# One core, a hybrid S5 and attention step: second products in two passes, and FFN heads that start on two of three chunks

## The chip, the cores and the metric

The kernel runs on one core of a Trainium2 chip. The metric is the device time of one execution in microseconds. TensorE (PE in the profile) multiplies, PEld is its weight load, VectorE is DVE, ScalarE is ACT, GpSimd is POOL; SP issues most of the DMAs.

## The reference

Two layers over 1024 latent and 256 context tokens, width 1024. Layer 0 mixes with an S5 state space model, whose result `z` goes through a gated product; layer 1 mixes with attention. Each is followed by a SwiGLU FFN of width 2816, and every sublayer ends in a residual and a LayerNorm:

```python
# S5 mixer, tail
val, gate = jnp.split(z @ w_glu, 2, axis=-1)
(val * jax.nn.sigmoid(gate)) @ w_out
# FFN
gate, up = jnp.split(h @ w_in, 2, axis=-1)
(jax.nn.silu(gate) * up) @ w_out
# around each sublayer
x = layer_norm(alpha * x + gate * sublayer(x * (1 + scale) + shift))
```

Latent tokens attend to latent and cached keys, context tokens to context alone. The outputs are `y`, the new keys and values, and the S5 end states.

## The kernel before, in words

The 1280 tokens lie along the free axis in three chunks, `CH`: chunks 0 and 1 are 512 latent tokens each, chunk 2 is the 256 context tokens. A [1024 x tokens] matrix is eight tiles of 128 partitions. Every product is three matmuls on numbers split in a high part `hi` and a rest `lo` (`mm3`: hi*hi, hi*lo, lo*hi): ACT copies to `hi`, and DVE, or POOL, subtracts to get `lo`. So each operand costs one ACT and one DVE or POOL instruction before PE can use it.

**First products** (S5 GLU, FFN in). The 2*NF output tiles come in gate and up pairs. The first one or two pairs (`ffn_head`) multiply all three chunks plainly, chunk by chunk as the LayerNorm gives them. The rest (`ffn_pair`) use a Winograd scheme on the latent chunks: seven products of 12 matmuls of 512 columns in place of eight, and two context products of 24 matmuls of 256 columns. It needs sums of weight blocks (S1 to S4, `i_step`, DVE) and sums of input tiles (T1 to T4, `x_sums`: a DVE subtraction, an ACT copy and a POOL subtraction, sixteen times). `x_sums` is handed out two or four at a time among the head units from chunk 1 on. Results are spilled to `dI`.

**Second products** (`out_chunks`: S5 out, attention out, FFN out) take three passes, one for each chunk, of eight output tiles `f`; each pass loads and splits all weights again (`w_ahead`), and splits the spilled tiles (`z_ahead`) during its first `f`. After a pass, that chunk's LayerNorm runs as a Python generator whose steps `boundary` emits between later units, by a clock of estimated PE time and the step lengths `YW`. The norm writes `hi` and `lo` of the next input at once (ACT and POOL); then `affine` forms the next residual (ACT for even tiles, POOL for odd), and `keep` stores it with a DMA of the SP queue. The residual tile of a unit is loaded on SP as the unit begins; in the S5 out product ACT scales it at once (`scaled`).

All engines run their instructions in the order in which they are written. Pages (512 columns) come from a pool of 88.

Of the kernel before, what the change touches and what calls it, by code (L numbers as in the profile page):

```python
# [6 lines left out]
F32 = mybir.dt.float32  # L7
# [6 lines left out]
P = 128  # L14
D = 1024
KT = 8
# [593 lines left out]
LL = 2.5  # L610


YW = (2.5, 3, 1, 4, 3.5, 1, 2.6)


class Dense(S5):
# [14 lines left out]
    def out_units(self, ws, tiles, acc, gate, c):  # L631

        v, g = self.nc.vector, self.nc.gpsimd
        n = len(tiles)
        ps = {}

        def mms(f, lo, hi):
            if lo == 0:
                ps[f] = self.psum()[:, :CH[c][1]]
            for i in range(lo, hi):  # L640
                t = tiles[i]
                self.mm3([ps[f]], *(x(P * f) for x in ws(i)), t[0][c:c + 1], t[1][c:c + 1], i == 0, i == n - 1)

        def unit(f, lo=0):
            mms(f, lo, n)
            self.accumulate(acc, gate, f, c, ps.pop(f))
            if f == 2:
                rs = self.rs[c] = self.pgn(CH[c][1])
                g.tensor_tensor(rs, acc[0][c], acc[1][c], op=ALU.add)
            for k in [f - 1] * (f > 2) + [f] * (f == 7):  # L650
                (v if k == 7 else g).tensor_tensor(self.rs[c], self.rs[c], acc[k][c], op=ALU.add)
            return 3 * n * CH[c][1] / 2400

        if c:
            return [lambda f=f: unit(f) for f in range(8)]

        first = [lambda f=f, i=i: mms(f, i, i + 1 + (i == 0)) for i in [0, *range(2, n - 1)] for f in range(4)]
        return first + [lambda f=f: unit(f, n - 1 if f < 4 else 0) for f in range(8)]

# [4 lines left out]


    def glu_plan(self, nt, cs, head, tail):

        ev = []
        done = 2 * head
        body = list(range(nt - tail))  # L670
        for a in range(0, len(body), cs):
            c = body[a:a + cs]

            need = max(done, min(2 * nt, 2 * c[-1] + 3))
            ev += [("in", (k // 2, k % 2)) for k in range(done, need)]
            done = need

            ev.append(((0, 1, 2) if c[-1] + 1 < nt - tail else (0,), c))
        return ev + [("in", (k // 2, k % 2)) for k in range(done, 2 * nt)]

    def glu_weights(self, win, wout, nt, cs, head, tail):
        out = [win[t] for t in range(2 * head)]
        for k, a in self.glu_plan(nt, cs, head, tail):
            out += [win[2 * a[0] + a[1]]] if k == "in" else [wout[t] for t in a]
        return out + [wout[t] for t in self.glu_last(nt, cs, tail)]

    def glu_gate(self, it, c, ps, half, act):

        n = CH[c][1]
        if half == 0:  # L690
            it["s"][c] = self.pgn(n)
            self.nc.scalar.activation(it["s"][c], ps, act)
        else:
            s = it["s"][c]
            self.nc.vector.tensor_tensor(s, s, ps, op=ALU.mult)
            for k in range(2):
                it["hl"][k][c] = self.pgn(n, F32R)
            self.split(it["hl"][0][c], it["hl"][1][c], s)

    def ffn_head(self, hh, hl, head, act, raw):  # L700

        ls, self.LS = self.LS, 0
        ws = [self.w_next() for _ in range(2 * head)]
        self.LS = ls
        s = {}
        sums = []

        def unit(t, half, c):
            n = CH[c][1]
            if c == 1 and t == half == 0:  # L710
                self.x_start(hh, hl, raw)
                sums.append(self.x_sums())
                self.i_load()
            ps = self.gemm(ws[2 * t + half], hh, hl, c)
            if half == 0:
                s[t, c] = self.pgn(n)
                self.nc.scalar.activation(s[t, c], ps, act)
            else:
                x = s.pop((t, c))
                self.nc.vector.tensor_tensor(x, x, ps, op=ALU.mult)  # L720
                self.spill(t, c, x)
            if sums:
                for _ in range(16 // (4 * head)):
                    next(sums[0], None)
            if c == 2:
                self.XC = [(hh[k][2], hl[k][2]) for k in range(KT)]
                self.i_until(2 * t + half + 2)
            return n / 100

        return [[lambda t=t, h=h, c=c: unit(t, h, c) for t in range(head) for h in range(2)] for c in range(3)]  # L730

    def glu_new(self, t):
        self.inter[t] = {"s": [None] * 3, "hl": ([None] * 3, [None] * 3)}
        return self.inter[t]

    def glu_head(self, hh, hl, head, act):

        self.inter = {}
        ls, self.LS = self.LS, 0
        ws = [self.w_next() for _ in range(2 * head)]  # L740
        self.LS = ls
        its = [self.glu_new(t) for t in range(head)]

        def unit(t, half, c):
            self.glu_gate(its[t], c, self.gemm(ws[2 * t + half], hh, hl, c), half, act)
            if c == 2:
                self.w_ahead(min(2 * t + half + 1, ls))
            return CH[c][1] / 100

        return [[lambda t=t, h=h, c=c: unit(t, h, c) for t in range(head) for h in range(2)] for c in range(3)]  # L750

    def glu_last(self, nt, cs, tail):

        return [*range(nt - tail, nt), *range(nt - tail - cs, nt - tail)]

    def glu_body(self, hh, hl, nt, cs, head, tail, act, acc, gate):
        for k, a in self.glu_plan(nt, cs, head, tail):
            if k == "in":
                t, half = a
                self.LS = LL if t == nt - 1 else 2  # L760
                it = self.inter[t] if half else self.glu_new(t)
                w = self.w_next()
                ps = self.gemm_all(w, hh, hl)
                for c in range(3):
                    self.glu_gate(it, c, ps[c], half, act)
            else:
                ws = [self.w_next() for _ in a]
                self.out_all(ws.__getitem__, [self.inter[t]["hl"] for t in a], acc, gate, k)

    def out_all(self, ws, tl, acc, gate, chunks=(0, 1, 2), each=None):  # L770
        for f in range(8):
            ps = [self.psum()[:, :CH[c][1]] for c in chunks]
            for i, t in enumerate(tl):
                rh, rl = ([t[k][c] for c in chunks] for k in range(2))
                self.mm3(ps, *(x(P * f) for x in ws(i)), rh, rl, i == 0, i == len(tl) - 1)
            for c, x in zip(chunks, ps):
                self.accumulate(acc, gate, f, c, x)
# [1317 lines left out]
```

## Time and profile before

| | |
|---|---|
| median of 3 runs (3427.3 to 3431.05) | 3430.57 us |
| the profiled execution's own time | 3426.6 us |
| its span, first to last instruction | 3424.8 us |
| mean granted TensorE clock, share of full speed | 0.965 |
| busy share: PE, PEld, DVE, ACT, POOL | 93%, 79%, 62%, 40%, 14% |

The profile is of one execution. A line such as L121 is the line of the kernel's source; L121, L123 and L125 are the three matmuls of `mm3`, L1079 those of a Winograd product and L1088 those of its context product. In a window the columns are its length, then for each engine the busy time with the number of instructions, then the granted clock of TensorE, the mean DMA share and GB/s.

### The profile page before, as it was taken

To read this page: it belongs to the slowest core of one execution; us is meant where nothing else is said; L and a number is where in the kernel's file an instruction comes from. 1 tells how busy PE (TensorE), PEld (TensorE's weight loads), DVE (VectorE), ACT (ScalarE), POOL (GpSimd) and SP (SyncE) were. 2 spreads that over 40 slices of the span, in tenths; PEclk is the share of its full clock that TensorE was granted. 3 is DMA by queue.
4 is the path that set the end of the run, shared out by engine and by line. 5 is a ranking of instruction groups with operands and counts; after the bars stand their busy time and mean duration, and the time that the engine had idled before them with its cause. 6 is when DMAs were issued, how large, how long until landed. Compare 5 with 4: busy or idle time off the path is not lost.

```text
span 3424.8 us, 47261 instructions
## 1 busy us (share of the span) xinstructions
PE 3199.5 (93%) x17734; PEld 2693.8 (79%) x17734; DVE 2109.5 (62%) x4279; ACT 1384.6 (40%) x2721; POOL 463.6 (14%) x435
## 2 busy tenths in 40 slices
PE   8999689997899999899889999999889999999997
PEld 5763568776788888787778899998678888878777
DVE  7789764475644444445555788887775444454645
ACT  3351442344422222424444477775453222232433
POOL 2230130032400000002122310001350000000000
PEclk9999789998999999999989999999899999999998
DMA  7679952334112121543442200002322121234544
GB/s 256 171 212 328 243 148 72 117 125 153 66 61 80 61 81 57 200 165 120 126 131 76 68 24 16 9 27 87 127 89 82 60 80 60 75 131 142 183 130 147
DMA packets 232998, 392.99 MB, mean 115 GB/s; under 512 B 54992, under 2 KB 111984, under 8 KB 232000
## 3 DMA queue, kind: packets, MB, share of 16 engines
q1 hardware_dynamic: 225280, 365.01, 33.4%
q0 software_dynamic: 7488, 24.96, 2.4%
q8 instruction: 139, 2.28, 0.3%
q14 instruction: 91, 0.75, 0.1%
HBM read 309.14 MB, written 80.74 MB: 114 GB/s over the span
## 4 chain that ended last, share of the span: by engine, by line
PE 74%; DVE 5%; ACT 2%; DMA 2%; issue 1%; POOL 1%; SPq 0%; ACTq 0%; DVEq 0%; POOLq 0%
PE ps L1079 26%; PE ps L123 9%; PE ps L121 9%; PE ps L125 9%; PE ps L1088 8%; PE ps L1478 3%; PE ps L1499 1%; PE ps L1497 1%; PE ps L1498 1%; PE ps L1436 1%; PE ps L1437 1%; PE ps L1438 1%; DVE pg L103 1%; ACT pg L102 1%; DMA pg<-dI 1%
## 5 line engine op out<-in xcount | busy, mean ns | idle before, releaser
L1079 PE MATMUL ps<-pg,pg 128*128 128x512 f32 x3948 | 919.3, 391 | 13.8 <-ACT pg L1102 8.6
L1079 PEld LDWEIGHTS ps<-pg,pg 128*128 128x128 f32 x3948 | 738.8, 189 | 165.5 <-ACT pg L1102 9.9
L121 PE MATMUL ps<-pg,pg 128*128 128x512 f32 (+1 forms) x2112 | 740.6, 370 | 103.1 <-ACT pg L131 65.1
L123 PE MATMUL ps<-pg,pg 128*128 128x512 f32 (+1 forms) x2112 | 731.7, 366 | 7.2 <-DVE pg L132 4.3
L125 PE MATMUL ps<-pg,pg 128*128 128x512 f32 (+1 forms) x2112 | 726.9, 364 | 6.0 <-DVE pg L103 5.9
L121 PEld LDWEIGHTS ps<-pg,pg 128*128 128x128 f32 x2112 | 407.8, 197 | 176.6 <-ACT pg L131 69.6
L123 PEld LDWEIGHTS ps<-pg,pg 128*128 128x128 f32 x2112 | 406.6, 197 | 76.1 <-DVE pg L132 11.9
L125 PEld LDWEIGHTS ps<-pg,pg 128*128 128x128 f32 x2112 | 406.9, 197 | 67.5 <-DVE pg L103 10.4
L103 DVE TENSOR_TENSOR pg<-wr,pg 128x512 fp32r<-128x512 f32 (+1 forms) x444 | 331.0, 788 | 182.2 <-ACT pg L102 178.2
L102 ACT ACTIVATE pg<-wr 128x512 fp32r<-128x512 f32 (+1 forms) x444 | 244.8, 597 | 325.4 <-DMA wr<-in_w_ffn_out 230.1
L1088 PEld LDWEIGHTS ps<-pg,pg 128*128 128x128 f32 x2256 | 283.1, 191 | 7.3
L1088 PE MATMUL ps<-pg,pg 128*128 128x256 f32 x2256 | 285.3, 283 | 0.0
L1204 POOL TENSOR_TENSOR pg<-pg,pg 128x512 f32<-128x512 f32 x8 | 11.6, 1450 | 1418.2 <-DVE pg L662 1336.0
L662 DVE SCALAR_TENSOR_TENSOR pg<-ps,mods,pg 128x512 f32<-128x512 f32 x64 | 47.9, 749 | 233.6 <-PE ps L125 226.3
L1044 DVE TENSOR_TENSOR pg<-pg,pg 128x512 fp32r<-128x512 f32 x188 | 137.8, 733 | 77.4 <-ACT pg L1040 77.4
L132 DVE TENSOR_TENSOR pg<-ps,pg 128x512 fp32r<-128x512 f32 (+1 forms) x210 | 142.0, 677 | 65.1 <-ACT pg L131 59.7
L131 ACT ACTIVATE pg<-ps 128x512 fp32r<-128x512 f32 (+1 forms) x210 | 124.0, 590 | 70.8 <-PE ps L1478 47.6
L1458 ACT ACTIVATE pg<-ps,nb,rq 128x512 f32<-128x512 f32 x192 | 149.0, 777 | 5.7 <-DVE sm L1467 2.6
L1127 DVE TENSOR_TENSOR pg<-pg,ps 128x512 f32<-128x512 f32 x47 | 32.3, 688 | 193.1 <-PE ps L1079 193.1
L1113 DVE TENSOR_TENSOR pg<-pg,ps 128x512 f32<-128x512 f32 x47 | 32.3, 688 | 191.2 <-PE ps L1079 191.2
L1443 DVE TENSOR_REDUCE mx<-ps 128x1 f32<-128x512 f32 (+1 forms) x208 | 137.0, 660 | 1.3 <-PE ps L1438 1.3
L1044 DVE TENSOR_TENSOR pg<-wr,pg 128x512 fp32r<-128x512 f32 x188 | 133.4, 709 | 2.2 <-ACT pg L1040 2.2
(344 smaller groups left out, 4707.3 us busy)
## 6 DMA issues: line engine op xcount, KB each, us to landing
gw<-in_w_mod SPq DMA_DIRECT2D x192, 256.0 KB, 5.2
wr<-in_w_ffn_out SPq DMA_DIRECT2D x96, 512.0 KB, 4.5
wr<-in_w_ffn_in SPq DMA_DIRECT2D x88, 512.0 KB, 4.1
dI<-pg SPq DMA_DIRECT2D x104, 256.0 KB, 4.6
pg<-dI SPq DMA_DIRECT2D x104, 256.0 KB, 5.4
wr<-in_w_ffn_out SPq DMA_DIRECT2D x48, 384.0 KB, 3.6
wr<-in_w_s_out SPq DMA_DIRECT2D x24, 512.0 KB, 3.6
dX<-pg SPq DMA_DIRECT2D x48, 256.0 KB, 2.5
```

The lines of the kernel that those rows point to most:

```text
L102: nc.scalar.activation(hi, x, AF.Copy)
L103: nc.vector.tensor_tensor(lo, x, hi.bitcast(F32), op=ALU.subtract)
L121: mm(ps[c], wh, rh[c], start=first, stop=False)
L123: mm(ps[c], wh, rl[c], start=False, stop=False)
L125: mm(ps[c], wl, rh[c], start=False, stop=last)
L131: self.nc.scalar.activation(hi, src, AF.Copy)
L132: self.nc.vector.tensor_tensor(lo, src, hi.bitcast(F32), op=ALU.subtract)
L1044: v.tensor_tensor(lo, self.isum[i, name], hi.bitcast(F32), op=ALU.subtract)
L1079: mm(ps, p[:, o], q, start=(first and k == 0 and j == 0), stop=(k == 3 and j == 2), skip_group_check=True)
L1088: mm(ps, p[:, o], q, start=(k == 0 and j == 0), stop=(k == KT - 1 and j == 2))
L1443: v.tensor_reduce(mx[:, kc:kc + 1], ps, axis=AX.X, op=ALU.max)
L1458: nc.scalar.activation(p, u["bank"].pop((qt, kc)), AF.Exp, bias=nb[:, 0:1], scale=rq, accum_out=sm[:, kc:kc + 1])
```

## The change

Every GLU and FFN pair is now Winograd (five plain pairs disappear: one in the GLU, two in each FFN). The first `GF` = 2 (GLU) or `FF1` = 3 (FFN) pairs are cut in two: `HEAD` (products P1 and P2, which read chunk 0 alone, and the context products G and U) and `TAIL` (the other five products, which read sums with chunk 1). The weights of such a pair are loaded twice.

Second products run in two passes (`TWO`): chunk 0 with the context, then chunk 1. The last FFN out product keeps three (`ONE`). Tiles are split ahead during the last pair (`last`). Residuals are loaded one `f` earlier, and scaled on ACT just before they are used.

The LayerNorm writes one plain tile; `h_split` splits it later, as do the hooks in the last unit of a pass, half of the `lo` on DVE and half on POOL. The T sums are formed by `x_next` as the first `TAIL` begins. `affine` issues its store on the queue of the engine that computed it (ACT or POOL), in place of SP.

```diff
-YW = (2.5, 3, 1, 4, 3.5, 1, 2.6)
+YW = (2.5, 3, 1, 4, 3.5, 1, 1.6)
...
             if A is not None:
-                t = self.pgn(n)
-                nc.scalar.activation(hh[kt][c], a, AF.Identity, bias=B[:, kt, cd:cd + 1], scale=A[:, kt, cd:cd + 1])
...
+                raw[kt][c] = t
                 if kt % 2:
                     v.tensor_scalar(t, a, A[:, kt, cd:cd + 1], B[:, kt, cd:cd + 1], op0=ALU.mult, op1=ALU.add)
                 else:
                     nc.scalar.activation(t, a, AF.Identity, bias=B[:, kt, cd:cd + 1], scale=A[:, kt, cd:cd + 1])
-                nc.gpsimd.tensor_tensor(hl[kt][c], t, hh[kt][c].bitcast(F32), op=ALU.subtract)
...
+            after(nc.gpsimd, kt, c)
...
+            after(nc.scalar, kt, c)
...
-        for c in range(3):
-            run(outs[c])
+        for units, cs in zip(outs, passes):
+            run(units)
             if not gens:
                 clock[1] = clock[0] + YW[0]
-            gens.append(ln(c, ready))
...
+            gens += [ln(c, ready) for c in cs]
+        for c, units in heads or ():
+            while not ready[c]:
+                clock[1] = clock[0] + step()
+            run(units)
...
+FULL = ("A11", "S1", "S2", "A12", "S3", "A22", "S4", "A21"), ("P1", "P5", "P6", "P2", "P7", "G", "P4", "P3", "U")
+HEAD = ("A11", "A12", "A21", "A22"), ("P1", "P2", "G", "U")
+TAIL = ("S1", "S2", "S3", "S4", "A22"), ("P6", "P5", "P7", "Z3", "P4")
...
+    def h_split(self, kt, c, eng):
...
+        self.nc.scalar.activation(hi, self.xr[kt][c], AF.Copy)
+        eng.tensor_tensor(lo, self.xr[kt][c], hi.bitcast(F32), op=ALU.subtract)
+        self.hs[kt, c] = hi, lo
+
+    def x_next(self, n):
...
+        eng = (v, g)[k % 2]
+        if n == "C":
+            self.h_split(k, 2, eng)
+        elif n[0] == "B":
...
+            self.h_split(kt, c, eng)
...
+            v.tensor_tensor(t, x, y, op=ALU.subtract)
+            self.xt[n, k] = t
+            hi, lo = self.page(F32R), self.page(F32R)
+            nc.scalar.activation(hi, t, AF.Copy)
+            eng.tensor_tensor(lo, t, hi.bitcast(F32), op=ALU.subtract)
+            self.X[n][k] = hi, lo
...
+        self.segs = [(t, HEAD) for t in p[:first]] + [(t, TAIL) for t in p[:first]] + [(t, FULL) for t in p[first:]]
...
+        h0 = [lambda: self.x_all("B11", "B21")] + [u for k, u in U[:2]]
+        h2 = [lambda: self.x_all("C")] + [u for k, u in U[2:]]
+        return [(0, h0), (2, h2)]
+
+    def ffn_body(self, act, first, last):
+        ready = {0: ("T1", "T2"), 1: ("T3",), 2: ("B22",), 3: ("T4",)}
+        for i in range(first, len(self.segs)):
+            for s, kind in enumerate(self.segs[i][1][1]):
+                if i == first:
+                    self.x_all(*ready.get(s, ()))
+                if i == len(self.segs) - 1:
+                    last(s)
+                self.ffn_step(i, kind, act)
...
+        self.zo = [(c, i) for cs in passes for i in range(nk) for c in cs]
...
+                for ps, x in zip(st["ps"], z):
+                    self.mm3([ps], *(y(P * (i - lo)) for y in w), x[:1], x[1:], i == 0, i == nk - 1)
...
+                        while hook and len(hook) > nh * (nk - 1 - i) / nk:
+                            hook.pop(0)()
...
+        TWO, ONE = ((0, 2), (1,)), ((0,), (1,), (2,))
+
+        def keep(eng, kt, c):
             o, n = CH[c]
-            nc.sync.dma_start(self.dX[kt][:, o:o + n], acc[kt][c])
...
+            eng.dma_start(self.dX[kt][:, o:o + n], acc[kt][c])
...
+        def last(s):
+
+            if s > 2:
+                self.z_ahead(2 * (s - 2))
+            if s > 3:
+                self.w_ahead(0.5 * (s - 3))
...
+        def ffn_hook(l):
+            self.x_start(new())
+            self.i_start(L("w_ffn_in", l), range(NF), FF1)
+            return some(0, ("B11", "B21"), 8) + [lambda k=k: self.i_until(k) for k in range(4)] + some(2, ("C",), 8)
...
+            for c in (0, 2, 1):
+                yield c, [lambda: take(c)] + h[c]
```

The last lines are the attention layer's heads: keys and values of chunk 0, then of the context, then of chunk 1, each after `take(c)` has split that chunk.

## Rows read from the trace of the kernel before

**Rows 1.** The page, part 1: busy time, share of the span, instructions of each engine.

```profile
PE 3199.5 (93%) x17734; PEld 2693.8 (79%) x17734; DVE 2109.5 (62%) x4279; ACT 1384.6 (40%) x2721; POOL 463.6 (14%) x435
```

**Rows 2.** Chain in order of time inside one pair: start us, us, what.

```profile
519.36 13.63 PE ps L1079 x60
532.99 2.87 PE ps L1088 x24
535.86 5.47 PE ps L1079 x24
```

**Rows 3.** Windows by stage: length, busy us (instructions) per engine, clock, DMA.

```profile
443.96:668.24 224.28, 210.37 (x1074) 179.12 (x1072) 127.83 (x184) 78.47 (x145) 30.92 (x18) 0.96 0.30 88
720.84:781.89 61.05, 50.91 (x211) 40.43 (x210) 40.92 (x68) 25.63 (x43) 20.77 (x17) 0.92 0.28 95
781.89:827.25 45.36, 32.43 (x211) 29.84 (x210) 30.12 (x61) 21.15 (x43) 5.63 (x8) 0.81 0.52 171
896.46:914.05 17.59, 15.45 (x62) 12.37 (x61) 12.75 (x17) 7.81 (x14) 12.25 (x8) 0.90 0.38 127
1397.22:1407.19 9.97, 0.17 (x3) 0.01 (x1) 2.14 (x20) 0.64 (x2) 0.00 (x0) 0.76 0.99 337
1530.23:1668.84 138.61, 128.88 (x548) 104.03 (x546) 71.16 (x119) 51.88 (x94) 23.61 (x18) 0.96 0.45 145
1668.84:1769.99 101.15, 81.55 (x574) 77.72 (x572) 64.29 (x113) 45.83 (x85) 20.15 (x18) 0.88 0.47 148
1769.99:1833.02 63.03, 58.18 (x382) 53.46 (x381) 37.44 (x79) 26.08 (x56) 17.00 (x19) 0.95 0.16 50
2351.26:2394.91 43.65, 43.65 (x195) 36.12 (x194) 27.14 (x38) 15.76 (x31) 9.64 (x6) 1.00 0.43 145
2394.91:2446.80 51.89, 47.43 (x212) 37.90 (x210) 41.30 (x67) 21.92 (x35) 19.09 (x14) 1.00 0.24 79
3062.83:3069.27 6.44, 0.17 (x3) 0.00 (x1) 0.46 (x3) 0.67 (x2) 0.00 (x0) 0.92 0.98 323
3191.98:3322.87 130.89, 125.07 (x548) 102.08 (x546) 66.03 (x115) 45.12 (x86) 9.33 (x6) 0.99 0.46 149
3322.87:3406.33 83.46, 73.18 (x548) 71.12 (x546) 53.19 (x102) 36.17 (x69) 5.98 (x6) 0.92 0.51 163
```

**Rows 4.** Waits of the SP queue at the stores: total us, times, longest.

```profile
SPq L1621 <- ACT pg L913: 135.8, 14, 22.2
...
SPq L1621 <- ACT hp L913: 77.4, 8, 40.4
```

**Rows 5.** Timeline of the SP queue in the first out product's second chunk.

```profile
770.68 2.26 SPq L1621 DMA_DIRECT2D dX<-pg  x2
773.02 0.38 SPq L1682 DMA_DIRECT2D pg<-in_x  x1
```

**Rows 6.** Timeline of ACT, same place; in brackets the idle time before, and releaser.

```profile
775.93 0.63 ACT L1683 ACTIVATE pg<-pg 128x512 f32<-128x512 f32 x1 [5.28 <-DMA pg<-in_x]
```

**Rows 7.** Timeline of ACT at the start of the S5 layer's GLU.

```profile
455.20 0.63 ACT L131 ACTIVATE pg<-pg 128x512 fp32r<-128x512 f32 x1 [0.34 <-DMA pg<-dZL]
```

**Rows 8.** Timeline of DVE in the GLU's first pairs.

```profile
479.83 2.48 DVE L989 TENSOR_TENSOR pg<-pg,pg 128x512 f32<-128x512 f32 x4
...
488.21 6.52 DVE L991 TENSOR_TENSOR pg<-pg,pg 128x512 f32<-128x512 f32 x4
```

**Rows 9.** Timeline of POOL over the same stretch.

```profile
478.84 22.06 POOL L995 TENSOR_TENSOR pg<-pg,pg 128x512 fp32r<-128x512 f32 x11 [3.90 <-ACT pg L994]
```

**Rows 10.** Groups by line and shape: busy us, mean ns, idle before, releaser.

```profile
L994 ACT ACTIVATE pg<-pg 128x512 fp32r<-128x512 f32 x48 | 28.8, 629 | 37.2 <-DVE pg L991 11.6 <-DVE pg L987 10.8 <-DVE pg L985 10.4
...
L995 POOL TENSOR_TENSOR pg<-pg,pg 128x512 fp32r<-128x512 f32 x48 | 75.2, 1593 | 62.7 <-ACT pg L994 62.7
```

**Rows 11.** Timeline of PE at chunk 2's norm before the first FFN.

```profile
860.01 0.59 PE L857 MATMUL ps<-hp,ones 128*128 128x256 f32 x2
...
880.14 0.58 PE L121 MATMUL ps<-pg,pg 128*128 128x256 f32 x1 [1.15 <-ACT pg L886]
```

More of the change, by code (lines that the diff above doesn't have):

```diff
@@ L629, in gemm_all @@
         return ps
[L631 to L658, printed above, removed]
     def accumulate(self, acc, gate, f, c, ps):
@@ L681, in glu_weights @@
[L681 to L750, printed above, removed]
@@ L770, in out_all @@
[L770 to L777, printed above, removed]
-            if each:
-                each()
@@ L898, in layer_norm @@
         ready[c] = True
-        if A is not None and after:
+        if A is not None:
             for kt in range(KT):
@@ L936, in run @@
                     clock[1] = max(clock[1], clock[0] - 2.0) + step()
-        for c in range(3):
-            run(outs[c])
+        for units, cs in zip(outs, passes):
+            run(units)
             if not gens:
                 clock[1] = clock[0] + YW[0]
-            gens.append(ln(c, ready))
-        hd = heads() if heads else [[], [], []]
-        for c in range(3):
-            if hd[c]:
-                while not ready[c]:
-                    clock[1] = clock[0] + step()
-            run(hd[c])
+            gens += [ln(c, ready) for c in cs]
[3 more added lines that the diff above has]
+            run(units)
         lap = 0
@@ new lines, in x_all, with i_start @@
+    def x_all(self, *names):
+        for n in names:
+            while self.x_next(n):
+                pass
+    def i_start(self, win, pairs, first):
+        self.win = win
+        p = list(pairs)
+        self.segs = [(t, HEAD) for t in p[:first]] + [(t, TAIL) for t in p[:first]] + [(t, FULL) for t in p[first:]]
+        self.items = [(i, n) for i, (_, (names, _)) in enumerate(self.segs) for n in names]
+        self.iraw, self.isum, self.ihi, self.isp, self.il, self.ik, self.iu = {}, {}, {}, {}, 0, 0, 0
+        self.ev = {}
@@ L1216 @@
+            return 3 * (hi - lo) * sum(CH[c][1] for c in cs) / 2220
+        return [[lambda p=p, f=f, o=o: unit(p, f, o) for f in range(8) for o in range(0, nk, 8)] for p in range(len(passes))]
 SHUF = [(i + 16) % 32 for i in range(32)]
@@ L1675, in rest @@
-        self.wseq += self.out_plan(L("w_s5_out"), KT)
-        zh = zl = None
-        body(AF.Sigmoid, KT, self.spilled)
+        self.x_start(zz)
+        for c in (0, 2, 1):
+            zload(c)
+        heads = self.ffn_heads(AF.Sigmoid, GF)
+        for c, units in heads:
+            for u in units:
+                u()
+        self.out_start(KT, TWO, self.spilled)
+        self.wseq += self.out_plan(L("w_s5_out"), KT, 2)
+        self.LS = 1.5
+        self.ffn_body(AF.Sigmoid, GF, last)
@@ new lines, in rest, with heads, take @@
+        self.x_start(new())
+        hooks = [lambda k=k: self.w_ahead(0.5 * k + 0.5) for k in range(8)]
+        outs = self.out_chunks(acc, self.mod(0, 5), NF, TWO, self.residual, None,
+                               some(0, ("B11", "B21"), 8) + hooks + some(2, ("C",), 8))
+        self.wseq += L("w_qk")[:2] + L("w_v") + L("w_qk")[2:]
+        hh, hl = new(), new()
+        def heads():
+            self.at_consts()
+            h = self.at_head(hh, hl)
+            def take(c):
+                for kt in range(KT):
+                    if (kt, c) not in self.hs:
+                        self.h_split(kt, c, (nc.vector, nc.gpsimd)[kt % 2])
+                    hh[kt][c], hl[kt][c] = self.hs[kt, c]
+            for c in (0, 2, 1):
+                yield c, [lambda: take(c)] + h[c]
```

456 lines of the change are left out of this document (204 added, 252 removed).

## The prediction

> **What bounds the kernel now.** First the page: PE is busy 93% of the span, no other engine above 62% (PEld apart) [rows 1]. So I ask what a stage costs over its matmuls. The chain of waits inside a Winograd pair gives the pace: 60 matmuls of 512 columns in 13.63 us are 0.2272 each, 24 of 256 in 2.87 are 0.1196, and a pair is 13.63 + 2.87 + 5.47 + 2.87 = 24.84 us with no gap [rows 2]. In the pairs PE is the bound. Then windows cut where stages meet, each against that pace [rows 3]. A chunk-1 pass of eight inputs needs 192 x 0.2272 = 43.6 us: the S5 out product took 61.1, the attention out product 51.9. A context pass needs 192 x 0.1196 = 23.0: 45.4 was taken. In the first FFN out product chunk 1 needs 120.0 and took 138.6, the context needs 63.1 and took 101.2. Out products begin with 10.0 and 6.4 us in which PE runs three matmuls. The loss lies at the joints.
>
> Why a pass loses: the SP queue waited 135.8 + 77.4 us at the stores of line 1621 for ACT's residual [rows 4]. In the S5 out product the residual load stands right behind two such stores, at 773.02 [rows 5]; ACT waited 5.28 us for it at 775.93, before the weight split in its queue [rows 6]. A context pass is short of split weights too: it splits as many as a latent pass in half the PE time.
>
> **The change, part by part.** *Pairs.* A plain pair is 48 matmuls a chunk, 48 x (2 x 0.2272 + 0.1196) = 27.55 us. Five become Winograd pairs: 5 x 2.71 = 13.6 us less PE work, contained in the stage sums below.
>
> *GLU* (443.96 to 668.24, 224.3 us [rows 3]). Eight pairs are 198.7. The first product waited for the first tile of z; now eight splits stand ahead of the first weight split on ACT, and z lands so slowly that the eighth copy ran at 455.20 [rows 7]. With 0.63 for it and as much for the weight, PE starts at 456.5, 12.5 us into the stage; I add 2.5 for the low clock after the gap (the stretch from 896.46 shows 0.90 of full speed over 17.6 us, 1.8 us [rows 3]). G waits for eight half-width splits: an ACT copy of 0.63 at full width and four POOL operations of 1.59 [rows 10], halved, about 4 us.
>
> Then the lump: T1 to T4 were spread over head units, and now stand at the first TAIL, in DVE's queue behind the last head's evacuation, which waits for PE. So nothing hides them. DVE has 16 differences, 10 `lo`, and some 9 operations for weights, at 0.62 [rows 8] 21.7 us; POOL has 10 `lo`. While POOL ran eleven in 22.06 us [rows 9], a DVE difference took 6.52/4 = 1.63 in place of 2.48/4 = 0.62 [rows 8]: each POOL operation costs DVE about one. So 32, and some 3.5 for waits on ACT, 35.5 against 13.6 of PE: 22 lost. Bounds: the 4 that the first body pair lost before an FFN (17.59 - 13.63 [rows 3]), and 47 if all 35 DVE operations ran at 1.7. I take 22, by the count of POOL operations. Stage: 198.7 + 12.5 + 2.5 + 4 + 22 = 239.7, **+15.4**.
>
> *S5 out and first FFN in* (668.24 to 1397.22, 729.0). The two-chunk pass needs 192 x 0.3468 = 66.6; weights are ready once per 8.3 us in place of 5.5 and 2.9, which hides their splits; 3 for its start. Chunk 1's pass: 52, as in the attention out product. By the clock of `boundary`, chunk 0's norm fills that pass's eight units (a step at each of the first ones), so the context's norm begins after P1, and must end before G. Before, its first matmul came at 860.01 and the context head at 880.14, 20.1 us [rows 11], and a plain chunk-1 head covered half. Now P2, 2.7 us, covers. I take the chain as 21.3 (T work gone from DVE, but a plain tile, a residual and a store come before the split): 18.6 idle and 3 of low clock, 21.5. Bounds 9 (most covered) and 25. Chunk 1's norm, under 28 us of later heads, still makes PE wait, 6. The lump: 22 + 5, since chunk 1's last scaling on DVE and four residuals and stores on ACT and POOL stand ahead. 22 pairs: 546.5. Sum 3 + 66.6 + 52 + 21.5 + 6 + 27 + 546.5 = 722.6, **-6.4**.
>
> *Attention out and second FFN in* (2351.26 to 3062.83, 711.6). The inputs were in SBUF, so the start gave nothing away; the same terms with 1.5 for the start: 721.1, **+9.5**.
>
> *First FFN out and the key and value heads* (1397.22 to 1833.02, 435.8). Here the second pass is 120 us and holds both norms. Start 1 (split ahead; the last pair hides it); pass 528 x 0.3468 = 183.1 and 4 for splits of two chunks' tiles in the first output (22 x 3 = 66 of 88 pages are held, unpriced in the trace: 0 to 15); chunk 1's pass 131, as in the last FFN out [rows 3]; heads 56.3 of matmuls and 12 of waits, where 63.0 were taken [rows 3] and the norm now ends late. Sum 387.4, **-48.4**. Bounds -30 and -60.
>
> *Last FFN out* (from 3062.83). Start 6.4 to 1, with its low clock -8; the SP queue freed of stores, -3 each in passes that took 130.9 and 83.5 [rows 3]: **-14**, bounds -6 and -20. Final stores change queue: an issue was 0.38 on SP [rows 5]; on ACT no row shows it, 0 to 1 each, beside the other engine's: 0.
>
> Elsewhere weights are read two times in place of three, at hidden cost; ACT's 12 store issues a joint lie under PE except in the lump (priced there).
>
> Sum: 15.4 - 6.4 + 9.5 - 48.4 - 14 = -43.9. From 3426.6 of the profiled execution that is 3382.7; the median of the other runs is 4 higher, so 3385, rounded.
>
> **The stores against a rule.** The rows show loads held behind stores [rows 4 to 6]. The Trainium skill, DMA: Bandwidth & Descriptors, Issuing engines are not separate DMA queues, says that starting DMAs on several engines "will only save the time on the sequencer it takes to initiate the DMA". By that rule the passes stay as long as they were; this trace disagrees as far as SP's waits go.
>
> **Rivals.** (1) *The sums and the context norm are covered.* If DVE reaches T1 early, lumps cost the 4 that the first body pair lost before [rows 3], 18 + 23 + 23 less, and two norm gaps of 9, 25 less: 3296. For: DVE is 62% busy. Against: program order, and a last head that waits for PE. (2) *Moving stores saves only their issue.* ACT waits for something else and the second passes stay at 61 and 139 (17 more), the last product's two gain nothing (6): 3408. For: no long store wait precedes every late weight. Against: rows 4 to 6. (3) *Slower: DVE and POOL hold each other through the whole first TAIL.* POOL then has residuals and stores pending besides its ten `lo`, every DVE operation takes 1.7, and each lump costs 47 or 52: 75 more, 3460. It decides from some 37 lost at each of the three places (+15 x 3 eats the gain). For: eleven POOL operations in a row did this [rows 8, 9]. Against: half of the `lo` moved to DVE.
>
> **How the numbers follow.** A measurement of this kernel tells about 0.2% (7 us) from nothing. Forecast with its own spread, 3355 to 3415: 0.47. Rival 1, wholly or in part, 3296 to 3355: 0.15. Rival 2, 3400 to 3423: 0.11. Rival 3, above 3437: 0.17. Mixtures that end within 7 us of 3430: 0.10. Faster 0.73, same 0.10, slower 0.17. The range 3335 to 3440 leaves out half of rival 1 and most of rival 3.
>
> **What would show it.** In the changed profile: no three-matmul window before the FFN out products; a two-chunk pass near 70 and 187 us; no SP wait at the residual stores; PE idle near 18 us between P2 and G before both FFNs, and none such before the keys' context head; a first TAIL of some 35 to 41 us in three places, its PE waiting for DVE and POOL `lo`; a GLU that starts 12 us late. The prediction is wrong if DVE gets to T1 while heads still run, if the two-chunk pass is held by pages, or if second passes still wait for loads.

## The result, and the profile after

The changed kernel took 3450.36 us (median of four runs, 3445.47 to 3455.31) beside 3428.94 us for the kernel before: ratio 1.0063, 95% interval 1.0045 to 1.0080, so 0.6% slower where 1.3% faster was forecast. The profiled execution took 3445.47 us, span 3443.4 against 3424.8. Part 1 of its page hardly differs from [rows 1]: PE is busy 3200.7 us, 93% again, VectorE 62% again. So the windows, by stage as in [rows 3], show it (length; busy us and instructions of PE, PEld, DVE, ACT, POOL; clock; DMA share; GB/s):

```profile
439.23:692.26 253.03, 215.91 (x1062) 180.23 (x1061) 134.96 (x204) 85.54 (x161) 24.05 (x20) 0.91 0.34 97
692.26:761.58 69.32, 67.72 (x386) 58.82 (x385) 33.53 (x48) 23.16 (x46) 14.64 (x12) 1.00 0.50 169
761.58:812.42 50.84, 47.03 (x214) 38.14 (x212) 40.91 (x69) 24.04 (x41) 13.34 (x14) 1.00 0.39 130
812.42:842.18 29.76, 11.20 (x34) 8.37 (x34) 22.75 (x51) 13.33 (x26) 6.65 (x7) 0.63 0.22 75
842.18:893.02 50.84, 35.49 (x210) 32.04 (x210) 38.30 (x71) 27.23 (x49) 15.28 (x20) 0.84 0.32 109
893.02:965.94 72.92, 65.94 (x239) 49.38 (x240) 51.39 (x72) 25.41 (x45) 12.29 (x9) 0.84 0.21 73
1424.28:1615.89 191.61, 189.01 (x1058) 162.02 (x1057) 70.30 (x114) 50.21 (x93) 15.03 (x12) 1.00 0.43 137
1615.89:1748.24 132.35, 126.22 (x558) 103.32 (x557) 84.12 (x154) 53.35 (x97) 27.05 (x26) 0.99 0.43 136
1748.24:1827.54 79.30, 69.10 (x415) 60.19 (x415) 58.20 (x103) 34.96 (x69) 23.34 (x25) 0.91 0.23 81
2346.71:3076.57 729.86, 685.43 (x3529) 584.53 (x3528) 410.15 (x668) 236.59 (x431) 62.55 (x60) 0.96 0.25 84
3200.93:3335.09 134.16, 127.33 (x547) 103.22 (x547) 65.84 (x115) 46.18 (x86) 9.31 (x6) 0.97 0.45 145
3335.09:3422.21 87.12, 74.36 (x545) 72.11 (x545) 53.17 (x100) 36.82 (x69) 5.97 (x6) 0.86 0.49 155
```

| stage, us | before | forecast | after |
|---|---|---|---|
| GLU | 224.3 | 239.7 | 253.0 |
| S5 out and first FFN in | 729.0 | 722.6 | 732.0 |
| first FFN out, k and v heads | 435.8 | 387.4 | 403.3 |
| attention out and second FFN in | 711.6 | 721.1 | 729.9 |
| last FFN out, to the span's end | 362.0 | 348.0 | 366.8 |

Out products no longer begin with three matmuls; the two-chunk passes took 69.3 and 191.6 us (forecast 69.6 and, with its start, 188.1); the chunk-1 passes 50.8 and 132.4 in place of 61.1 and 138.6. What they gained went at the joints. From P1 to G before the first FFN (812.42 to 842.18) PE was busy 11.2 of 29.8 us at a mean clock of 0.63. The rest of the heads (842.18 to 893.02, the wait for the first sums included) took 50.8 for matmuls that need 28.1. The window of the first TAILs (893.02 to 965.94: the three TAILs and the first five products of the pair behind them) took 72.9 for 240 matmuls that need 54.5. And the last product's passes got longer: 134.2 and 87.1 for 130.9 and 83.5 [rows 3].

Two timelines say how. In the GLU (PE, then ACT; idle time before and its releaser in brackets) G begins after 9.78 us in which PE waited for the context's copies; ACT had these behind the next pair's weight copies, which waited 12.89 us for their load, issued behind 24 loads of z:

```profile
452.11 1.22 PE L946 MATMUL ps<-pg,pg 128*128 128x512 f32 x2 [11.90 <-ACT pg L906]
...
470.94 8.27 PE L956 MATMUL ps<-pg,pg 128*128 128x256 f32 x48 [9.78 <-ACT pg L825]
```
```profile
466.51 1.15 ACT L906 ACTIVATE pg<-wr 128x512 fp32r<-128x512 f32 x2 [12.89 <-DMA wr<-in_w_s_glu]
...
470.49 2.54 ACT L825 ACTIVATE pg<-pg 128x256 fp32r<-128x256 f32 x8
```

In the context's pass of the last out product, ACT does all of chunk 1's final scalings (L752) and now issues their stores (ACTq L1525). ACT stands idle some 0.42 us between two scalings, 0.34 of it the store's issue, and the weight copies (L102) stand behind them all: from 3373.71 to 3381.09 six scalings with their stores take 7.4 us. PE, from 3374.6, waits 7.19 us:

```profile
3378.24 0.34 ACTq L1525 DMA_DIRECT2D out_y<-pg  x1
3378.63 0.81 ACT L752 ACTIVATE pg<-pg,lnb,lng 128x512 f32<-128x512 f32 x1 [0.42 <-ACT pg L752]
...
3381.09 1.15 ACT L102 ACTIVATE pg<-wr 128x512 fp32r<-128x512 f32 x2 [0.41 <-ACT pg L752]
```
```profile
3381.77 0.58 PE L121 MATMUL ps<-pg,pg 128*128 128x256 f32 x1 [7.19 <-ACT pg L102]
```

### The profile page after: what moved, and what is told of

The parts are those of the page before. It is cut to its first block, busy times and chain, and to the rows that moved or that the text cites. A ratio compares the mean times of both kernels' runs of the same rounds, so it can differ in the third digit from the quotient of the medians.

```text
span 3443.4 us, 46852 instructions
## 1 busy us (share of the span) xinstructions
PE 3200.7 (93%) x17674; PEld 2678.0 (78%) x17674; DVE 2126.4 (62%) x4317; ACT 1350.6 (39%) x2667; POOL 402.4 (12%) x420
## 4 chain that ended last, share of the span: by engine, by line
PE 76%; DVE 12%; issue 4%; ACT 3%; DMA 3%; SPq 1%; POOL 1%; ACTq 0%; DVEq 0%; POOLq 0%
PE ps L946 27%; PE ps L123 9%; PE ps L121 9%; PE ps L125 9%; PE ps L956 8%; PE ps L1375 2%; DVE sw L537 1%; PE ps L1396 1%; PE ps L1395 1%; PE ps L1394 1%; PE ps L1333 1%; PE ps L1334 1%; PE ps L1335 1%; DVE X L543 1%; DVE sw L541 1%
## 5 line engine op out<-in xcount | busy, mean ns | idle before, releaser
L946 PE MATMUL ps<-pg,pg 128*128 128x512 f32 x4368 | 1053.7, 399 | 81.4 <-ACT pg L851 43.7
L946 PEld LDWEIGHTS ps<-pg,pg 128*128 128x128 f32 x4368 | 830.8, 193 | 273.6 <-ACT pg L851 50.9
L121 PE MATMUL ps<-pg,pg 128*128 128x512 f32 (+1 forms) x1872 | 639.7, 364 | 33.8 <-ACT pg L131 18.9
L123 PE MATMUL ps<-pg,pg 128*128 128x512 f32 (+1 forms) x1872 | 634.0, 361 | 5.7 <-DVE pg L132 3.7
L125 PE MATMUL ps<-pg,pg 128*128 128x512 f32 (+1 forms) x1872 | 629.1, 358 | 0.2 <-DVE pg L103 0.2
L121 PEld LDWEIGHTS ps<-pg,pg 128*128 128x128 f32 x1872 | 349.9, 191 | 98.6 <-ACT pg L131 23.3
L123 PEld LDWEIGHTS ps<-pg,pg 128*128 128x128 f32 x1872 | 349.7, 191 | 65.1 <-DVE pg L132 9.2
L125 PEld LDWEIGHTS ps<-pg,pg 128*128 128x128 f32 x1872 | 349.5, 191 | 52.8 <-DVE pg L103 1.3
L956 PE MATMUL ps<-pg,pg 128*128 128x256 f32 x2496 | 323.2, 287 | 21.4 <-ACT pg L825 21.4
L956 PEld LDWEIGHTS ps<-pg,pg 128*128 128x128 f32 x2496 | 319.6, 196 | 30.0 <-ACT pg L825 22.4
L102 ACT ACTIVATE pg<-wr 128x512 fp32r<-128x512 f32 x344 | 192.0, 597 | 362.7 <-DMA wr<-in_w_ffn_out 168.0
L103 DVE TENSOR_TENSOR pg<-wr,pg 128x512 fp32r<-128x512 f32 x344 | 261.2, 798 | 102.8 <-ACT pg L102 91.3
L910 DVE TENSOR_TENSOR pg<-wr,pg 128x512 fp32r<-128x512 f32 x216 | 154.5, 719 | 24.4 <-ACT pg L906 24.4
L131 ACT ACTIVATE pg<-ps 128x512 fp32r<-128x512 f32 (+1 forms) x210 | 123.3, 588 | 67.8 <-PE ps L1375 47.6
L906 ACT ACTIVATE pg<-wr 128x512 fp32r<-128x512 f32 x216 | 132.1, 620 | 14.6 <-DMA wr<-in_w_s_glu 12.9
```

Source lines behind the costliest of these rows:

```text
L102: nc.scalar.activation(hi, x, AF.Copy)
L103: nc.vector.tensor_tensor(lo, x, hi.bitcast(F32), op=ALU.subtract)
L121: mm(ps[c], wh, rh[c], start=first, stop=False)
L123: mm(ps[c], wh, rl[c], start=False, stop=False)
L125: mm(ps[c], wl, rh[c], start=False, stop=last)
L131: self.nc.scalar.activation(hi, src, AF.Copy)
```

## Experiments

Each time is a median beside runs of the kernel before on the same chip, which lay between 3426.8 and 3429.4 us. Edits are against the changed kernel where nothing else is said.

**1. Without the sums** (x1), in `x_next`:

```diff
+            self.X[n][k] = self.hs[k + 4 * (n[1] in "24"), 0]
+            return True
```

> The changed kernel without the sums T1 to T4 (48 differences, copies and lo's at three places are left out; their products read chunk 0's tiles instead, so part of the result is not computed). Theory: the lumps of 26, 32 and 32 us at the first TAIL of the three first products are these sums, uncovered, so each falls to 4 to 10: 3370 to 3395 us. Rival: the lumps are mostly the backlog of chunk 1's norm, stores and weight splits, and the sums only stand in it: 3425 to 3440 us.

3364.6 us, 86 less, 5 below the theory's band. The windows from P1 to G, of the rest of the heads, and of the first TAILs before the first FFN:

```profile
782.36:811.89 29.53, 11.09 (x34) 8.21 (x34) 22.74 (x51) 13.32 (x26) 6.64 (x7) 0.63 0.22 75
811.89:848.05 36.16, 33.55 (x209) 30.33 (x210) 28.58 (x56) 19.07 (x37) 9.51 (x14) 0.93 0.29 98
848.05:908.07 60.02, 56.33 (x243) 46.17 (x242) 41.08 (x63) 23.81 (x41) 7.34 (x7) 0.97 0.34 121
```

The first is as it was; the heads got 14.7 shorter and the TAILs 12.9, at a clock of 0.97. With 86 us in all, the lumps are the sums for the most part. Not all of it need be: without the sums four of a TAIL's five products no longer read chunk 1, so a wait for that chunk's norm goes with them. In the changed kernel VectorE begins the first difference at 883.91, 3.6 us after PE's last head.

**2. Norms that may lag 8 us** (x2), in `boundary`: `clock[0] - 2.0` becomes `clock[0] - 8.0` where there are heads.

> The changed kernel with one number changed: the norms' emission may lag 8 us behind the matmuls' in place of 2, at the joints with heads. Theory: the 24 us between P1 and G before both FFNs are lost because that cap keeps the context's norm from being issued in the chunk-1 pass, though the pass has room for it; so each gap falls to under 8, and chunk 1's norm starts earlier too: 3395 to 3420 us. Rival: the norms of two chunks are bound by VectorE and ScalarE in that pass, so the wait only moves into the pass or before P1: 3440 to 3455 us.

3451.0: no gain. The chunk-1 pass and P1 to G:

```profile
764.21:824.60 60.39, 52.58 (x222) 41.63 (x221) 50.18 (x95) 30.23 (x54) 18.39 (x18) 0.92 0.33 118
824.60:844.04 19.44, 9.93 (x30) 7.02 (x29) 13.93 (x28) 10.46 (x18) 5.28 (x8) 0.73 0.45 135
```

The gap lost 10.3 us and the pass gained 9.6: the rival held, and the first FFN out's second pass too went from 132.4 to 142.3. One reason can be read on DVE and POOL: four `lo` of chunk 0 run on POOL through the norm's square root, and operations of two columns take 1.2 us in place of 0.16.

```profile
820.84 1.22 DVE L677 SCALAR_TENSOR_TENSOR rs<-rs,rs 128x2 f32<-128x2 f32 x1
...
823.34 0.16 DVE L676 TENSOR_TENSOR rs<-rs,rs 128x2 f32<-128x2 f32 x1
```
```profile
818.26 5.04 POOL L827 TENSOR_TENSOR pg<-pg,pg 128x512 fp32r<-128x512 f32 x4
```

**3, 4. Stores back on SP**: the final ones (x3), or all (x4).

```diff
-            eng.dma_start(self.O["y"][kt][:, o:o + n], acc[kt][c])
+            nc.sync.dma_start(self.O["y"][kt][:, o:o + n], acc[kt][c])
```

> The changed kernel with the 24 final stores back on the SP queue, the joints' stores left on ACT and POOL. Theory: in the last out product weight splits stand on ACT behind eight stores that each wait for ACT's own result; that cost PE 7 us near the start of the context's pass, which goes: 3441 to 3445 us. Rival (a store costs its queue only its issue, and eight issues of 0.34 us hide): no change, 3448 to 3452 us.

> The changed kernel with all stores of the residual and of the result back on the SP queue, as in the kernel before. Theory: SP waits again at the residual's stores, and residual and weight loads behind them come late in the second passes: 10 us over the version with only the final stores on SP, 3450 to 3460 us. Rival: the queues were never a cause and the stores on ACT and POOL lie in the norms' and lumps' way, so it gains: 3425 to 3440 us.

3438.6 and 3423.5: 12 and 27 less (x3 passes its theory's band by 2 us, x4 its rival's by 2), the second level with the kernel before (0.9990, 0.9979 to 1.0001), by the rival that moved stores stand in the way. Of x4, P1 to G, the last product's second and third passes, the largest of SP's waits at the residual's stores, and two rows of ACT:

```profile
821.60:845.85 24.25, 11.31 (x34) 8.49 (x34) 17.77 (x49) 13.22 (x26) 3.60 (x3) 0.64 0.31 110
3191.38:3321.10 129.72, 125.21 (x548) 102.26 (x547) 66.02 (x115) 45.36 (x86) 9.33 (x6) 0.99 0.47 150
3321.10:3401.98 80.88, 71.70 (x545) 69.84 (x544) 52.52 (x100) 36.19 (x69) 5.99 (x6) 0.94 0.52 166
```
```profile
SPq L1521 <- ACT pg L752: 112.5, 13, 44.6
```
```profile
821.29 1.15 ACT L906 ACTIVATE pg<-wr 128x512 fp32r<-128x512 f32 x2 [3.89 <-DMA wr<-in_w_ffn_in]
...
3357.33 4.34 ACT L752 ACTIVATE pg<-pg,lnb,lng 128x512 f32<-128x512 f32 x6 [1.36 <-DVE pg L718]
```

SP waits at the stores again, 112.5 us in this row, as it did in [rows 4]; the kernel is 27 us faster all the same. On ACT the six scalings of the last product now take 4.3 us in place of 7.4, and PE waits 2.9 us behind them in place of 7.2. At the joints two things meet. From P1 to the out product the FFNs take 604.0 and 602.2 us for 611.9 and 612.3, but P1 comes 5.0 and 3.7 us later, counted from the start of the out product before it. Before the first FFN ACT waits 3.89 us there for a weight load, the first behind four stores in SP's queue (812.56 to 817.40). So SP's waits still cost something, and less than the stores on ACT and POOL do.

**5. One-chunk passes in the first FFN out** (x5): `TWO` becomes `ONE` for that product, its weights are planned three times, its heads run in the order 0, 1, 2.

> The changed kernel with the first FFN out product back in three passes of one chunk (heads in the order of chunks 0, 1, context), all else kept. Theory: the two-chunk pass saves some 21 us of passes there (the last FFN out product, still in three passes, took 124 + 134 + 87 = 345, this one 192 + 132 = 324), and some of it is lost again in the heads, whose norms end late: 3455 to 3466 us. Rival: the pass brought the whole gain of this stage, 32 us: 3478 to 3490 us.

3469.1, 19 more: 3 over the theory's band and 9 below the rival's. The stage took 418.3 for 403.3, so the merged pass is worth 15 there.

**6. Low parts on VectorE** (x6): `eng = (v, g)[k % 2]` becomes `eng = v`.

> The changed kernel with every low part of the late splits and of the sums on VectorE (half of them were on GpSimd). Theory: where VectorE and GpSimd share such a run, the VectorE operations stretch from 0.6 us to 2 and more, so that GpSimd's half is slower than VectorE alone; four 8 us stretches before P1 and the three first TAILs get shorter: 3425 to 3440 us. Rival: VectorE is the busier engine there and its 36 extra operations at three places cost what the lock cost: 3445 to 3460 us.

3450.1: no change, the rival's number. Before the first FFN PE's wait inside P1 for a weight's low part fell from 5.1 to 1.6 us, and the one before the first TAIL grew from 13.0 to 15.1: what the lock of experiment 2 cost, the extra VectorE operations cost. So the run does not say what the lock alone is worth.

**7. The kernel before with the stores moved** (x7): in its `affine`, `after(kt, c)` becomes `after(eng, kt, c)`, and both stores use `eng.dma_start`.

> The kernel before with one part of the change alone: the stores of the residual and of the result issued on ACT and POOL behind the operation that makes them. Theory (formed from the version with all stores on SP, 27 us faster than the changed kernel): each store makes ACT wait for its own result, ahead of weight splits, and SP's waits cost little, so this is slower than before: 3437 to 3455 us. Rival (the prediction's step): the loads behind SP's stores made the second passes late, so this is faster than before: 3390 to 3415 us.

3405.9, 23 less: my new theory missed, the prediction's step held. From chunk 0's mean product to the context's, in the S5 out, first FFN out, attention out and last out products:

```profile
724.13:847.08 122.95, 109.91 (x541) 92.13 (x540) 84.34 (x143) 64.33 (x110) 49.30 (x46) 0.93 0.39 136
1523.80:1741.65 217.85, 197.82 (x1094) 172.09 (x1093) 135.65 (x228) 98.08 (x178) 50.99 (x44) 0.95 0.48 155
2372.00:2489.35 117.35, 103.32 (x541) 87.12 (x540) 86.57 (x143) 58.28 (x95) 50.19 (x46) 0.99 0.41 139
3161.00:3379.65 218.65, 196.59 (x1071) 171.19 (x1069) 117.32 (x213) 82.97 (x155) 15.28 (x12) 0.93 0.46 149
```

The kernel before took 133.7, 234.1, 126.8 and 208.9 between the same matmuls: three places gained 36, the last lost 10. So the move has two signs, by place (experiment 18).

**8. Sums in the heads** (x8). Behind `ready[c] = True` in `layer_norm`, and four at a time between the GLU's last head units:

```diff
+        if c == 1 and self.sums:
+            while self.t_next():
+                for _ in range(1):
+                    self.t_next()
+                yield 1.3
```

> The changed kernel with the sums T1 to T4 issued as soon as their chunk is ready: between the last head units before the GLU, and right behind chunk 1's scaling, ahead of its residual work, before both FFNs. Theory: the sums were late by their place in the queues alone: the GLU's lump of 26 falls by 12 to 20, those of the FFNs by 3 to 8 each (chunk 1 itself is ready late): 3418 to 3435 us. Rival: VectorE has no room in the heads either, and the heads' evacuations wait behind the sums: 3445 to 3460 us.

3448.0: within the scatter, the rival's number but not its reason. From the GLU's P1 to its out product it took 234.9 for 240.4, at the FFNs nothing, for there chunk 1 is ready when the heads are over (at 881.98): the row of PE with its norm's last product before the first FFN, ahead of the scaling on VectorE and ACT, and the first product of the first TAIL:

```profile
875.10 1.13 PE L691 MATMUL ps<-ident,rstd 128*128 128x128 f32 x8 [2.36 <-DVE rstd L677]
...
893.76 0.80 PE L956 MATMUL ps<-pg,pg 128*128 128x512 f32 x1 [11.78 <-ACT pg L856]
```

**9. The GLU's order** (x9): one weight tile ahead in place of `AHEAD` = 4 until the context is split.

> The changed kernel; in the GLU's first head units only one weight tile is split ahead in place of four, so that the context's copies come before those of the second pair's weights on ACT. Theory: G waits 9.8 us there because these copies stand behind a weight load that was issued behind 24 loads of z (ACT waited 12.9 us for it); without that the gap falls to 1 to 3 us: 3438 to 3443 us. Rival: the context's own tiles are not ready earlier, or the first TAIL takes back what G gains: 3447 to 3453 us.

3440.7, 9.6 less, as the theory had it. G's wait is now 1.82 us:

```profile
462.38 8.36 PE L958 MATMUL ps<-pg,pg 128*128 128x256 f32 x48 [1.82 <-ACT pg L827]
```

**10. Fillers** (x10): `matmul(ps[:, :P], self.ident, self.ident)`, 12 to 80 at a place.

> The changed kernel with idle matmuls of the identity (nothing reads them) put into PE's queue where it waits: before P1, G and the first TAIL in the GLU, and before P1, around the context norm's two small products and before the first TAIL at both FFNs, each 50 to 70% of the idle time there. Theory: after each of these waits PE runs at the lower of its two clocks for 10 to 20 us, which costs about 11 + 14 + 14 us; with PE kept busy most of that goes: 3415 to 3435 us. Rival: at a low clock PE is only late for work that VectorE and ScalarE bring late anyway, so nothing changes, or the fillers themselves cost a little: 3446 to 3460 us.

3445.6, beside 3450.4: inside the scatter. From P1 to G, the rest of the heads, the first TAILs before the first FFN:

```profile
823.19:849.64 26.45, 25.88 (x204) 24.46 (x204) 20.55 (x54) 11.41 (x25) 4.37 (x7) 1.00 0.25 81
849.64:897.77 48.13, 44.02 (x310) 40.74 (x309) 35.68 (x68) 25.03 (x41) 12.99 (x18) 0.96 0.34 113
897.77:970.08 72.31, 64.25 (x240) 48.06 (x241) 51.47 (x72) 25.34 (x45) 12.22 (x9) 0.88 0.24 73
```

The clock is 1.00 and 0.96 of full speed in the first two, where the changed kernel had 0.63 and 0.84, and they took 26.5 and 48.1 for 29.8 and 50.8. But P1 itself came later by more: from the S5 out product's start to the first TAIL it took 202.3 for 200.8. The TAILs took 72.3 for 72.9. So far as the low clock stands ahead of the TAILs, it goes with the waits and costs little. Inside them, where the clock fell again (0.88), the runs don't part the two.

**11, 12. All together** (x11: 4, 6, 8, 9, the lag of 2, and the context split ahead of its residual work), **and with five first pairs** (x12):

```diff
-GF, FF1 = 2, 3
+GF, FF1 = 2, 5
```

> The changed kernel with all of this together: stores on SP, the GLU's order of copies, sums as early as their chunk is ready, the context's splits ahead of its residual work, every low part on VectorE, and norms that may lag 8 us. Theory: the parts add up (27 for the stores, 9 for the GLU's order, 6 for its sums), and early emission helps now that no store stands in ACT's and POOL's queues: 3375 to 3400 us. Rival: at the joints VectorE and ScalarE are full whatever the order, so only the stores and the GLU count: 3405 to 3420 us.

> The combined kernel with five first pairs in place of three before both FFNs. Theory: two more pairs of heads (22 us of matmuls that need no sums) cover the sums that three don't, 20 us at each FFN are less by 10 to 15: 20 to 30 us below the combined version. Rival: a first TAIL needs more of VectorE per matmul than a full pair (A22 is split again, Z3 adds once more), so two more of them give back what the cover gains: within 8 us of the combined version.

3421.9 and 3396.6. P1 to G, the rest of the heads, the first TAILs, of x11 and then of x12:

```profile
817.18:826.42 9.24, 6.93 (x29) 4.77 (x28) 8.85 (x20) 2.69 (x6) 1.71 (x4) 1.00 0.17 58
826.42:873.49 47.07, 34.05 (x208) 31.30 (x208) 37.35 (x74) 25.10 (x47) 6.53 (x5) 0.84 0.26 82
873.49:955.56 82.07, 62.70 (x240) 49.04 (x241) 54.66 (x87) 30.63 (x54) 0.00 (x0) 0.82 0.28 100
```
```profile
822.48:830.63 8.15, 7.10 (x31) 4.94 (x29) 7.90 (x18) 2.52 (x5) 1.67 (x3) 1.00 0.20 65
830.63:911.69 81.06, 61.28 (x350) 55.20 (x351) 60.51 (x114) 42.60 (x78) 5.53 (x5) 0.85 0.31 103
911.69:993.97 82.28, 82.14 (x363) 67.48 (x362) 56.30 (x91) 28.93 (x51) 0.00 (x0) 1.00 0.33 112
```

In x11 the gap at G is down from 24.3 (x4) to 9.2, and the first TAILs up from 72.5 to 82.1: what was late is now late elsewhere, for a net of 7. The lag also cost 12 in the first FFN out (411.3 against x4's 399.5), so the parts did not add up and both bands were missed. With two more pairs of heads the TAILs run at pace, 360 x 0.2274 = 81.9 and took 82.3, at full clock: the theory's number held. The wait did not all go, though. The heads' window took 81.1 us for matmuls that need 50.5, and PE waits there for VectorE, which now forms the sums: 5.97 us for chunk 1's norm, 4.84 and 8.63 for a weight's low part.

```profile
895.35 5.07 PE L971 MATMUL ps<-pg,pg 128*128 128x256 f32 x22 [8.63 <-DVE pg L925]
```

From P1 to the out product the changed kernel loses 65 us over its 546.5 of matmuls, x12 34.

**13 to 15.** Cover alone (x13: the line above in the changed kernel); more of it (x14: `GF, FF1 = 4, 6`); x12 with its stores on ACT and POOL (x15).

> The changed kernel with five first pairs in place of three before both FFNs and nothing else. Theory: cover alone does not help, because the sums T1 to T4 are issued only at the first TAIL, behind the last head, however many heads there are; only the waits on chunk 1's own scaling go: 3438 to 3450 us. Rival: the lump was the norm's and the stores' backlog on VectorE and ScalarE, which drains under more heads: 3420 to 3432 us.

> The combined kernel with six first pairs before both FFNs and four in the GLU (five and two in the version before it, 3397 us). Theory: each further first pair still hides some 4 us at each FFN and the GLU's two hide 8 of its lump: 3378 to 3390 us. Rival: first TAILs are bound by VectorE, more of them only stretch it: 3394 to 3408 us.

> The combined kernel with five first pairs (3397 us with its stores on SP) and the stores on ACT and POOL. Theory: a store still holds ACT until its own result is out, ahead of weight splits, in the last out product and at the joints: 3412 to 3424 us. Rival: with cover at the joints only the last product's 11 us come back: 3404 to 3410 us.

3432.1, 3382.5 and 3417.7. Cover alone brings 18, the edge of the rival's band: some of the loss was backlog that drains. x14 is the fastest version, 0.9868 of the kernel before (0.9848 to 0.9888); its gain over x12 is the GLU's, 221.4 for 236.1, while from P1 to the out product the FFNs took 582.5 and 582.1 for 580.1 and 583.2, so there the sixth pair gave nothing. x15, in the theory's band: the stores cost 21 here too. Of x14, the GLU from P1:

```profile
460.21:681.60 221.39, 206.83 (x1055) 178.04 (x1056) 132.23 (x219) 81.86 (x154) 0.00 (x0) 0.95 0.34 106
```

**16, 17. Residual loads**: one output earlier in the kernel before (x16); back with their own output in x4 (x17).

```diff
-                acc[f][c] = self.pgn(n)
-                residual(acc[f][c], f, c)
+                for k in [0] * (f == 0) + [f + 1] * (f < 7):
+                    acc[k][c] = self.pgn(n)
+                    residual(acc[k][c], k, c)
```

> The kernel before with its residual loads issued one output earlier, stores still on SP. Theory: the stores on SP cost PE time there because the residual load of the output in work stands right behind them; with it issued one output earlier most of the 23 us that moving the stores gave comes here too: 3402 to 3415 us. Rival: the weight loads behind the stores are what comes late, and they stay: 3424 to 3433 us.

> The changed kernel with all stores on SP (3423 us) and its residual loads issued with the output itself, as in the kernel before. Theory: the early loads are what made SP's store waits harmless, so 10 to 20 us come back: 3433 to 3443 us. Rival: they were harmless because of the two-chunk pass and the z tiles loaded ahead: 3420 to 3428 us.

3420.4 and 3425.8: 7 less than before, between the two bands, and 2 more than x4, the rival's. Late residual loads are some 7 of the 38 us that the residual's stores on SP cost the kernel before (experiment 18), and nothing that can be told from the scatter in the changed one.

**18. Only the residual's stores moved** (x18): x7 with its final stores on SP.

> The kernel before with the residual's stores on ACT and POOL, the final stores still on SP (3406 us with both moved, 3428 with none). Theory: the residual's stores gain where three one-chunk passes wait for loads behind them, the final ones only cost ACT's queue, 8 to 12 us: 3393 to 3400 us. Rival: the final stores' move is neutral and the last product was longer for another reason: 3402 to 3410 us.

3389.2, 0.9896 of the kernel before (0.9876 to 0.9916), 4 us better than the theory's band. The last product is back where it was (208.9). PE's waits for ACT's splits of the spilled tiles (L131) and of the weights (L102), in the kernel before and then in x18, show most of what was gained:

```profile
PE ps L121 <- ACT pg L131: 65.1, 16, 9.8
PE ps L121 <- ACT pg L102: 32.3, 12, 7.1
```
```profile
PE ps L121 <- ACT pg L131: 49.5, 14, 9.8
PE ps L121 <- ACT pg L102: 19.8, 8, 5.8
```
```profile
3159.80:3368.90 209.10, 192.83 (x1070) 168.74 (x1068) 116.75 (x213) 81.34 (x155) 15.32 (x12) 0.96 0.47 155
```

## Why the prediction was wrong

By the profiles the sum was to be 44 less and came out 19 more. Of the 63 between, 13 lie in the GLU, 9 in each of the two stages that hold an out product and the FFN's first products, 16 in the first FFN out and 19 in the last one, less 4 outside. With the stores back on SP (x4) 13 are left in the GLU, 7 and 2 in those two stages, 12 in the first FFN out and 6 in the last one.

*The step that failed first is the stores'.* The prediction read SP's waits as the cause of late second passes, gave -3 to each pass of the last product, 0 to the final stores, and let ACT's issues "lie under PE". Its mechanism holds in the kernel before: the residual's stores alone, moved, bring 38 us there, 28 of them seen in PE's waits for splits of spilled tiles and weights, whose loads SP issues too (x18). There the Trainium skill's rule (DMA: Bandwidth & Descriptors, Issuing engines are not separate DMA queues: only the sequencer's time to initiate a DMA is saved) fell short: what was saved is the wait of what stands behind a store in an in-order queue. But in the changed kernel the move cost more than it saved: with its stores on SP it is 27 us faster by the medians (x4), 21 by the two profiles. Of these, 13 lie in the last product, to the span's end, 4 in the first FFN out, and 3 and 6 from the out product before each FFN to the one behind it; before the GLU 4 go the other way. What was overlooked is that the wait does not vanish. It moves to ACT, where each scaling with its store takes some 0.5 us more (7.4 for 4.3 us in six), ahead of weight and context copies that PE needs next. SP's waits do some harm in the changed kernel too (the 3.89 us of x4). Why they do so much less than in the kernel before stays open: it is not the earlier residual loads (x16, x17). That a weight tile serves two chunks and is needed less often fits, and was not tried alone.

*GLU, G waits "about 4".* Mis-sized: 9.8. The count was of the eight splits and left out what ACT had ahead of them, a weight copy with a load behind 24 others; without that order the kernel is 9.6 faster, and G's wait 8.0 shorter (x9). The start (12 late), the lump (26 for 22) and the pairs were near.

*The lumps.* That nothing hides the sums was right, and the size short: forecast 22 + 27 + 27, by the stage rows 26 + 32 + 32, and 86 when the sums are left out (x1). The way to that size was wrong. The prediction counted VectorE operations and let each GpSimd one hold VectorE for one more, so that PE would wait for the low parts. In the TAILs' row 72 VectorE operations took 51.4 us, 0.71 each, and over the whole kernel PE waited for ACT's copies of the sums (L851) far longer than for POOL's low parts (L852):

```profile
PE ps L946 <- ACT pg L851: 43.7, 8, 13.0
...
PE ps L946 <- POOL pg L852: 8.6, 15, 0.9
```

What sets the lump is, by these rows, the chain at the joint, VectorE and ScalarE in turn: a difference, its copy, its low part. Of the 21.5 us in which VectorE stood idle in that window some 9 ended with an ACT operation and 11 with PE. Waits moved when the order changed (x2, x11) and shrank when more matmuls covered them (x12). How much of the chain is hand-offs and how much work is not parted. Nor is the clock: of the 18.4 us lost in that window PE stood idle for 7.0, and its 65.9 busy us for matmuls that need 54.5 are for the most part the low clock (0.84 of full speed in the row).

Rival 1, that the sums hide, is wrong for three first pairs and right in part for five with early sums (x12). Rival 3 named the outcome, slower, by a cause that this trace does not show: it wanted 1.7 us for every VectorE operation. (Its upper bound of 47 is 46 by its own numbers, 35 x 1.7 - 13.6.) With the low parts of these sums off POOL nothing changed (x6), though that run also loads VectorE. The lock itself is as the Trainium skill has it (SBUF — State Buffer, Who interferes with whom: a VectorE operation with two SBUF inputs contends with a GpSimd one that reads SBUF); the 1.22 us for a two-column operation agree.

*The context's norm.* "21.5" was 24.3 by the window from P1 to G, in part by luck: 5.1 of it is P1's own wait for a weight's low part, which the sum did not have, and from the end of P2 (826.78) to G 15.7 went, for 18.6 of idle time forecast.

```profile
818.55 4.64 PE L946 MATMUL ps<-pg,pg 128*128 128x512 f32 x10 [5.12 <-DVE pg L910]
```

Its cause, program order alone, was wrong: earlier emission moved most of the wait into the pass (x2) or the TAILs (x11).

*First FFN out.* -32.5 for -48.4: the pass 191.6 for 188.1, chunk 1's 132.4 for 131 and the heads 79.3 for 68. Why the heads are 11 longer was not followed. The merged pass itself is worth 15 to 19 (x5).

*Right:* no stall at the starts, both passes, the late GLU, PE idle before G, none of SP's stores among its waits. *Not tried:* what it costs that the weights of a first pair are loaded and split twice, for which the sum has no term of its own.

## What to carry to other kernels

A store costs most on the queue where something urgent stands behind it, and an issue behind its own engine's result holds that engine (some 0.5 us each here): choose the queue place by place, and price both the queue that is freed and the one that is burdened. Before putting work off until the last chunk is ready, count the vector and scalar work that then falls into one joint, and give PE matmuls that need none of it: here two more first pairs were worth 25 us (18 in the changed kernel as it was), where reordering at the FFNs moved the waits and won at most 7. A wait that moves when its work is issued earlier points to a full chain; one that goes, as G's in the GLU did (x9), was bad order.

## What was not expected of the hardware

PE's clock was raised ahead of the TAILs without a gain (x10). In the five-pair version the first TAILs ran at 1.00 (2.4 GHz) with no filler, where three pairs had 0.82 to 0.88: there the clock followed the waits.
